# One scheduler step more ahead of two groups of TensorE products in a two-layer hybrid decoder trunk

## The chip, the cores and the metric

The kernel runs on one core of one Trainium2 chip. The metric is the device time of one execution in microseconds (us). Before the change it is 919.61 us, the median of three runs (918.66 to 920.67).

## What is computed

Each of two layers normalises x (256 tokens, 2048 channels), projects it to the inputs of four head groups, computes each group, gates it, and maps the four back through `w_out` with a residual. The change touches the attention groups (fox, moba) and the gated linear attention (gla). Cut from the reference:

```python
def hybrid_layer(x, layer_idx, norm_g, w_in, ..., w_out, rope_diff, rope_moba):
    h = rms_norm(x, norm_g)
    p = split_columns(jnp.einsum("bsd,de->bse", h, w_in))
    fox = forgetting_attention(...)      # softmax(q k^T * scale + F[t] - F[s], causal) v
    diff = differential_attention(...)   # (softmax(q1 k1^T) - lam softmax(q2 k2^T)) v
    moba = moba_attention(...)           # with 256 tokens: one causal block, softmax(q k^T) v
    gla = gla_chunked(...)               # S_t = diag(a_t) S_{t-1} + k_t^T v_t,  o_t = q_t S_t
    mixed = jnp.concatenate([fox, diff, moba, gla], axis=-1)
    return x + jnp.einsum("bse,ed->bsd", mixed, w_out)

def reference(x, ...):
    for l in range(DEPTH):               # DEPTH = 2, SEQ = 256, D_MODEL = 2048
        x = hybrid_layer(x, l, ...)
    return rms_norm(x, final_norm_g)
```

The kernel does not evaluate gla chunk by chunk as the reference does. It splits the 128 tokens of a row block into seven levels (halves, quarters, down to single tokens). At each level the keys of a first half, scaled by their decay to the middle, meet the queries of the second half, scaled by their decay from the middle, in one 128x128 product. These seven are called the **level products** here.

## The kernel before

**The main stream.** All the weights of both layers pass through one loop, `for i, s in enumerate(plan)`. A step holds two 128-row slices of weights, 512 columns wide (some blocks have 348, the last ones 256). An SP DMA brings it to `raw` (four buffers); ScalarE rounds it to `hi`, VectorE subtracts to `lo` (four buffers each, prepared three steps ahead); TensorE multiplies twelve times: both row blocks of x with `hi`, of the low part of x with `hi`, and of x with `lo`. `load` starts the DMA of step i+7 in iteration i, `prepare` the split of step i+3. A layer has 128 steps of `w_in` and 32 of `w_out`, plus the narrow last column block in layer 1. Steps are counted from 0 in this text, and steps of layer 1 from 160.

**The side work.** Everything else (softmax, rotations, gates, gla) is written as Python generators, the tasks. After the twelve multiplications of step i the loop calls `tick`, which runs each task to its next `yield`, unless the estimated cost of VectorE's or ScalarE's side work is over the time that TensorE's work has given (`left`); then the rest of the tasks get no turn in this iteration. So a `yield` puts what follows it one iteration later at least. The order of instructions on every engine is fixed when the program is built, and each engine works its own list in that order. VectorE's side work of iteration i stands behind the `lo` of step i+3, TensorE's behind the multiplications of step i.

**gla (L591).** For each of two pairs of heads it makes seven decays on VectorE (tile `eight`), their exponentials on ScalarE, the scaled queries on VectorE (`tq`, fourteen small products, a `yield` inside), then the scaled keys on VectorE (seven products into `eight`, L654 to 656). After a `yield`, VectorE does two last products for the state (L658, L659), and in that same turn, without a `yield`, TensorE's level products for row block 0 (`matmul(pc[:, i], ee[:, m, i], tq[:, m, i], ...)`, L664) are issued. Row block 1 and the state's product follow one iteration apart. `pcs` and `px` are PSUM tiles named `side`, of which there are two.

**attend (L742), used by fox and moba.** The probabilities of each row block are turned by `turned_p`: a transposition of 32x32 squares on VectorE, four SP DMAs to DRAM (`far`), one POOL DMA back (`four<-far`, or `two<-far` for row block 0), and then four yields (`LANDS`). `attend` waits for both, yields once (L762), and issues twelve products with v (L766 to 770): for each head one from `two` and two from `four`. The result is gated on VectorE and split to `mTh` (ScalarE) and `mTl` (VectorE), the left operands of `w_out`. The first eight steps of `w_out` use the quarters of gla and fox, the next four diff's, and only then, from the thirteenth step (step 140) on, moba's.

**Pools.** Tiles `four` (ten slots), `two` (six), `eight` (one), `side` (two), `far` (six) are handed out in the order in which they come free. A task that finds none waits an iteration.

Of the kernel before, what the change touches and what calls it, by code (L numbers as in the profile page):

```python
# [207 lines left out]
def hybrid_trunk(  # L208
# [83 lines left out]
    def joined(box):  # L292
        while not box:
            yield
        return box[0]
# [295 lines left out]
    def gla(l, an):  # L591
        yield from until("constants")
        ps = yield from take_side()
        for m in range(2):
            transpose(ps[0:16, m * P:(m + 1) * P], an[:, m])
        yield
        v_.tensor_copy(at17[0:16], ps[0:16, 0:256])
        side.put(ps)
        yield
        al = yield from take_side()  # L600
        for pair in range(2):
            matmul(al[:, pair * SEQ:(pair + 1) * SEQ], wa[:, l, pair * P:(pair + 1) * P], at17, True, True)
        yield
        e = yield from s2.take([P, 512])
        gl = yield from s2.take([P, 2, SEQ])
        yield from log_sigmoid(gl.rearrange("p a t -> p (a t)"), al[:, :512], e)
        s2.put(e)
        side.put(al)
        yield

        F = yield from s2.take([P, 2, 2, P])
        for pair in range(2):
            for m in range(2):
                v_.tensor_tensor_scan(F[:, pair, m], one.to_broadcast([P, P]), gl[:, pair, m * P:(m + 1) * P], 0.0,
                                      op0=OP.mult, op1=OP.add)
        s2.put(gl)
        yield from until(("gla_qk", l))
        qkT = env["gla_qk", l]
        dgs = env["dgs", l].rearrange("p m h -> p (m h)")
        sT = yield from s4.take([P, 2, H, P])  # L620
        for c in range(8):
            a_.activation(sT[:, c // 4, c % 4], ident, AF.Copy, scale=dgs[:, c:c + 1])
        sx = yield from s2.take([P, H, P])
        for pair in range(2):
            ee = yield from s8.take([P, 2, NL + 1, P])

            for i, h in enumerate(GLA_LEVELS):
                f = F[:, pair].rearrange("p m (b two h) -> p m b two h", two=2, h=h)
                z = ee[:, :, i].rearrange("p m (b two h) -> p m b two h", two=2, h=h)
                mid = f[:, :, :, 0, h - 1:h].to_broadcast([P, 2, 64 // h, h])  # L630
                v_.tensor_sub(z[:, :, :, 0], mid, f[:, :, :, 0])
                v_.tensor_sub(z[:, :, :, 1], f[:, :, :, 1], mid)
                if i % 3 == 2:
                    yield
            v_.tensor_sub(ee[:, 0, NL], F[:, pair, 0, P - 1:].to_broadcast([P, P]), F[:, pair, 0])
            yield
            a_.activation(ee[:, 0], ee[:, 0], AF.Exp, scale=1.0 / GLA_TAU)
            a_.activation(ee[:, 1, :NL], ee[:, 1, :NL], AF.Exp, scale=1.0 / GLA_TAU)
            a_.activation(ee[:, 1, NL], F[:, pair, 1], AF.Exp, scale=1.0 / GLA_TAU)
            yield  # L640

            def half(z, h, second):
                return z.rearrange("p m (b two h) -> p m b two h", two=2, h=h)[:, :, :, second]

            qv, kv = (qkT.rearrange("p (m c) t -> p c m t", m=2)[:, c] for c in (pair, 2 + pair))
            for i, h in enumerate(GLA_LEVELS):
                for hh in range(2):
                    rows = slice(hh * 64, hh * 64 + 64)
                    v_.tensor_mul(tq[rows, :, i, hh].rearrange("p m (b h) -> p m b h", h=h), half(ee[rows, :, i], h, 1),
                                  half(qv[rows], h, 1))  # L650
                if i == 3:
                    yield
            yield
            for i, h in enumerate(GLA_LEVELS):  # L654
                dst = half(ee[:, :, i], h, 0)
                v_.tensor_mul(dst, dst, half(kv, h, 0))
            yield
            v_.tensor_mul(ee[:, 0, NL], ee[:, 0, NL], kv[:, 0])  # L658
            v_.tensor_mul(ee[:, 1, NL], ee[:, 1, NL], qv[:, 1])  # L659
            for m in range(2):  # L660
                pcs = yield from take_side()
                pc = pcs.rearrange("p (l x c) -> p l x c", l=NL + 1, x=2)
                for i in range(NL):
                    matmul(pc[:, i], ee[:, m, i], tq[:, m, i], True, True)  # L664
                yield
                for i, h in enumerate(GLA_LEVELS):
                    if h >= 32:
                        for k in range(0, P, 2 * h):
                            a_.activation(sT[k:k + h, m, pair * 2:pair * 2 + 2, k + h:k + 2 * h],
                                          pc[k:k + h, i, :, k // 2:k // 2 + h], AF.Copy)  # L670
                        continue
                    dst = sT[:, m, pair * 2:pair * 2 + 2].rearrange("p x (b two h) -> p x b two h", two=2, h=h)[:, :, :, 1]
                    src = pc[:, i].rearrange("p x (b h) -> p x b h", h=h)
                    mk = masks[:, i].rearrange("p (b h) -> p b h", h=h)[:, None].to_broadcast([P, 2, 64 // h, h])
                    v_.copy_predicated(dst, mk, src)
                side.put(pcs)
            px = yield from take_side()
            for hh in range(2):
                rows = slice(hh * 64, hh * 64 + 64)
                matmul(px[:, hh * 512:hh * 512 + P], ee[rows, 0, NL], ee[rows, 1, NL], True, True, tiles=2)  # L680
            s8.put(ee)
            yield
            a_.activation(sx[:, pair * 2:pair * 2 + 2], px.rearrange("p (h t) -> p h t", h=2)[:, :, :P], AF.Copy)
            side.put(px)
        s4.put(qkT)
        s2.put(F)
        yield from until(("gla_v", l))
        yield
        vn = env["gla_v", l]
        ops = yield from take_side()  # L690
        o = ops.rearrange("p (m h d) -> p m h d", m=2, h=H)
        for h in range(H):
            matmul(o[:, 0, h], sT[:, 0, h], vn[:, 0, h * P:(h + 1) * P], True, True)
        for h in range(H):
            matmul(o[:, 1, h], sT[:, 1, h], vn[:, 1, h * P:(h + 1) * P], True, False)
            matmul(o[:, 1, h], sx[:, h], vn[:, 0, h * P:(h + 1) * P], False, True)
        s4.put(sT, vn)
        s2.put(sx)
        yield
        yield from finish_rows(l, 3, o, ops, None, env["gla_sg", l], gng[:, l:l + 1])  # L700
# [41 lines left out]
    def attend(l, gi, name, qT, kT, forget=None):  # L742

        su = sm.tile([P, 2, H], F32, name="su")
        rs = sm.tile([P, 2, H], F32, name="rs")
        boxes = []
        for m, pool in enumerate((s2, s4)):
            p = yield from softmax_part(m, qT, kT, slice(0, P), HD ** -0.5, su, forget)
            if m:
                s4.put(qT, kT[0])  # L750
                if forget is not None:
                    forget.release()
            v_.reciprocal(rs[:, m], su[:, m])
            for h in range(H):
                a_.activation(p[:, h], p[:, h], AF.Copy, scale=rs[:, m, h:h + 1])
            yield
            boxes.append(spawn(turned_p(p, m, partial(pool.put, p))))
        yield from until((name + "_v", l))
        yield from until((name + "_g", l))
        t0, p0 = yield from joined(boxes[0])  # L760
        t1, p1 = yield from joined(boxes[1])
        yield  # L762
        vn, (sgt, sg) = env[name + "_v", l], env[name + "_g", l]
        ops = yield from take_side()
        o = ops.rearrange("p (m h t) -> p m h t", m=2, h=H)
        for h in range(H):  # L766
            v0, v1 = (vn[:, j, h * P:(h + 1) * P] for j in range(2))
            matmul(o[:, 0, h], v0, p0[:, h], True, True)
            matmul(o[:, 1, h], v0, p1[:, 2 * h], True, False)
            matmul(o[:, 1, h], v1, p1[:, 2 * h + 1], False, True)  # L770
        s2.put(t0)
        s4.put(t1, vn)
        yield
        mixed = yield from s4.take([P, 2 * H, P])
        v_.tensor_mul(in_squares(mixed), ops.rearrange("p (x i r) -> p x i r", i=4, r=32), sg)
        side.put(ops)
        s4.put(sgt)
        yield
        yield from split_group(l, gi, mixed)
# [511 lines left out]
```

## Time and profile before

| | |
|---|---|
| median of three runs | 919.61 us |
| the profiled execution: its own time | 920.54 us |
| its span, first to last instruction | 918.8 us |
| TensorE busy | 901.3 us (98%) |
| VectorE busy | 571.5 us (62%) |
| ScalarE busy | 524.6 us (57%) |
| mean granted TensorE clock | 0.995 |
| DMA | 205.34 MB, 223 GB/s over the span |

In the profile PE is TensorE, PEld its weight load, DVE VectorE, ACT ScalarE, SPq SyncE's queue. L178 is the helper through which all VectorE and ScalarE instructions pass, and L276 the one of all matmuls, so the tile names tell them apart: `mm<-hi,hTp` and `mm<-lo,hTp` are main-stream steps (`mTh`, `mTl` in `w_out`), `side<-tq,eight` the level products, `side<-two,four` and `side<-four,four` the products with v. An fp32 matmul that is not split counts as two records. A timeline row has the start, the length, the engine, the instruction and its count; in brackets at its end stands the engine's idle time ahead of it, and what ended it.

### The profile page before, as it was taken

The page shows a single profiled execution, that of the slowest core. Times are in us where ns is not written, and L with a number is a line of the kernel's source. Part 1 is how long each engine was busy: PE and PEld are TensorE (multiplying, and loading weights), DVE is VectorE, ACT ScalarE, POOL GpSimd, SP SyncE. Part 2 cuts the span into 40 slices and gives each one's busy share as a digit, 9 for nine tenths or more (in the row PEclk, how much of TensorE's full clock was granted, in tenths as well). Part 3 has the DMA queues.
Part 4 walks back from the last instruction along what each step waited for, and adds up shares of the span by engine and source line. Part 5 has one row for each costly group of instructions (what it writes and reads, how often), then busy time and mean ns, then how long its engine had stood idle before and what let it go on. Part 6 is the DMA issues. An engine that isn't in the chain of part 4 may idle for free.

```text
span 918.8 us, 12421 instructions
## 1 busy us (share of the span) xinstructions
PE 901.3 (98%) x4490; PEld 766.8 (83%) x4490; DVE 571.5 (62%) x831; ACT 524.6 (57%) x819; POOL 38.6 (4%) x55
## 2 busy tenths in 40 slices
PE   8999999999999999999999999999999999999996
PEld 6988789888888888888899887988888888878886
DVE  6765887566558556555655568856655674565662
ACT  6588654664455556535565784566444654754441
POOL 0000000000000010000000000010000000110000
PEclk9999999999999999999999999999999999999998
DMA  8767656587656947757776466667877687587652
GB/s 264 255 206 263 234 182 240 167 301 263 233 183 205 319 156 236 276 200 259 235 231 212 145 235 194 192 212 213 290 231 228 172 264 274 159 307 254 193 164 92
DMA packets 77455, 205.34 MB, mean 223 GB/s; under 512 B 9265, under 2 KB 29137, under 8 KB 77394
## 3 DMA queue, kind: packets, MB, share of 16 engines
q1 hardware_dynamic: 70496, 183.44, 60.7%
q0 software_dynamic: 5408, 19.40, 6.1%
q10 hardware_dynamic: 1490, 1.71, 0.6%
q8 instruction: 35, 0.57, 0.2%
q14 instruction: 26, 0.21, 0.1%
HBM read 184.07 MB, written 20.45 MB: 223 GB/s over the span
## 4 chain that ended last, share of the span: by engine, by line
PE 86%; DMA 4%; ACT 3%; DVE 2%; issue 2%; SPq 1%; DVEq 0%; POOLq 0%; POOL 0%; ACTq 0%
PE mm L276 77%; PE side L276 9%; DMA four<-far 3%; DMA far<-four 1%; ACT hi L178 1%; ACT four L178 1%; DVE lo L178 1%; SPq L310 1%; DMA raw<-in_weights 1%; ACT L178 0%; DVE four L178 0%; DVE tq L178 0%; DVE eight L178 0%; ACT two L178 0%; DVE two L178 0%
## 5 line engine op out<-in xcount | busy, mean ns | idle before, releaser
L178 DVE TENSOR_TENSOR lo<-raw,hi 128x1024 fp32r<-128x1024 f32 (+1 forms) x316 | 368.4, 1170 | 305.4 <-ACT hi L178 288.5
L178 ACT ACTIVATE hi<-raw 128x1024 fp32r<-128x1024 f32 (+1 forms) x316 | 319.1, 1017 | 301.6 <-PE mm L276 244.1
L276 PE MATMUL mm<-hi,hTp 128*128 128x512 f32 (+1 forms) x1920 | 461.3, 382 | 2.6 <-ACT hi L178 2.6
L276 PEld LDWEIGHTS mm<-hi,hTp 128*128 128x128 f32 x1920 | 352.3, 188 | 68.1 <-ACT hi L178 3.9
L276 PE MATMUL mm<-lo,hTp 128*128 128x512 f32 (+1 forms) x960 | 248.3, 380 | 0.0
L276 PEld LDWEIGHTS mm<-lo,hTp 128*128 128x128 f32 x960 | 177.8, 188 | 32.7
L276 PE MATMUL mm<-hi,mTh 128*128 128x512 f32 (+1 forms) x256 | 64.6, 377 | 0.0
L276 PE MATMUL mm<-hi,mTl 128*128 128x512 f32 (+1 forms) x256 | 64.4, 376 | 0.0
L276 PE MATMUL mm<-lo,mTh 128*128 128x512 f32 (+1 forms) x256 | 64.4, 376 | 0.0
L276 PEld LDWEIGHTS mm<-lo,mTh 128*128 128x128 f32 x256 | 46.2, 188 | 8.8
L276 PEld LDWEIGHTS mm<-hi,mTl 128*128 128x128 f32 x256 | 46.2, 188 | 8.7
L276 PEld LDWEIGHTS mm<-hi,mTh 128*128 128x128 f32 x256 | 46.1, 188 | 8.7
L312 POOL DMA_DIRECT2D four<-far x32 | 17.2, 538 | 617.2 <-DMA far<-four 266.3
L276 PE MATMUL side<-four,four 128*128 128x128 f32 (+1 forms) x320 | 37.3, 277 | 1.9 <-DMA four<-far 1.9
L276 PEld LDWEIGHTS side<-four,four 128*128 128x128 f32 (+1 forms) x320 | 34.1, 190 | 4.6 <-DMA four<-far 2.5
L178 DVE STREAM_TRANSPOSE four<-four 128x1024 f32<-128x1024 f32 x24 | 29.5, 1230 | 0.0
L178 ACT ACT_TABLE_LOAD x22 | 28.2, 1283 | 0.3
L178 ACT ACTIVATE four<-mm,rstd 128x512 f32<-128x512 f32 (+1 forms) x40 | 24.4, 661 | 0.1
L276 PE MATMUL side<-hi,hTp 128*128 128x348 f32 x128 | 22.9, 321 | 0.0
L178 ACT ACTIVATE four<-side 32x64 f32<-32x64 f32 (+2 forms) x28 | 8.8, 342 | 24.3 <-PE side L276 24.3
L276 PEld LDWEIGHTS side<-hi,hTp 128*128 128x128 f32 x128 | 20.8, 188 | 1.3 <-issue 0.7
L178 ACT ACTIVATE four<-side,nb 128x256 f32<-128x256 f32 (+1 forms) x48 | 20.4, 437 | 1.5 <-DVE nb L178 1.2
(135 smaller groups left out, 500.1 us busy)
## 6 DMA issues: line engine op xcount, KB each, us to landing
raw<-in_weights SPq DMA_DIRECT2D x272, 512.0 KB, 4.3
far<-four SPq DMA_DIRECT2D x128, 128.0 KB, 4.2
four<-far POOLq DMA_DIRECT2D x32, 512.0 KB, 6.4
raw<-in_weights SPq DMA_DIRECT2D x47, 348.0 KB, 3.4
xs<-in_x SPq DMA_DIRECT2D x4, 512.0 KB, 5.1
four<-in_xt SPq DMA_DIRECT2D x3, 512.0 KB, 5.6
far<-two SPq DMA_DIRECT2D x24, 64.0 KB, 3.6
two<-far POOLq DMA_DIRECT2D x6, 256.0 KB, 5.2
```

Of the source, the lines that this page charges most:

```text
L178: return f(*args, **kw)
L276: t_.matmul(out, lhsT, rhs, start=start, stop=stop)
L310: nc.sync.dma_start(d[:, :, i].rearrange("j c f -> c j f"), t[32 * i:32 * i + 32].rearrange("c (j f) -> c j f", j=4))
L312: g_.dma_start(t, d.rearrange("j c i f -> (j c) (i f)"))
```

## The change

A `yield` is added at two places. In `gla`, the level products move to the turn after the two last VectorE products, and with them all that follows in the task. In `attend`, the products with v and what follows move one turn back. No instruction is added or taken away in the source.

```diff
@@ -657,6 +657,7 @@ (gla)
             yield
             v_.tensor_mul(ee[:, 0, NL], ee[:, 0, NL], kv[:, 0])
             v_.tensor_mul(ee[:, 1, NL], ee[:, 1, NL], qv[:, 1])
+            yield
             for m in range(2):
                 pcs = yield from take_side()
                 pc = pcs.rearrange("p (l x c) -> p l x c", l=NL + 1, x=2)
@@ -759,6 +760,7 @@ (attend)
         yield from until((name + "_g", l))
         t0, p0 = yield from joined(boxes[0])
         t1, p1 = yield from joined(boxes[1])
+        yield
         yield
         vn, (sgt, sg) = env[name + "_v", l], env[name + "_g", l]
         ops = yield from take_side()
```

TensorE, layer 0, the first pair of heads: `hi_1017` belongs to step 40, `hi_1043` to step 41. Before:

```order
L276 MATMUL mm_1101<-hi_1017,hTp_113 128x512 x8
L276 MATMUL mm_1101<-lo_1018,hTp_113 128x512 x4
L276 MATMUL side1_1116<-tq_94,eight0_900 128x128 x7
L276 MATMUL mm_1101<-hi_1043,hTp_113 128x512 x8
L276 MATMUL mm_1101<-lo_1044,hTp_113 128x512 x4
L276 MATMUL side0_1150<-tq_94,eight0_900 128x128 x7
```

Of the change, at the same place of TensorE's list:

```order
L276 MATMUL mm_1101<-hi_1017,hTp_113 128x512 x8
L276 MATMUL mm_1101<-lo_1018,hTp_113 128x512 x4
L276 MATMUL mm_1101<-hi_1043,hTp_113 128x512 x8
L276 MATMUL mm_1101<-lo_1044,hTp_113 128x512 x4
L276 MATMUL side1_1134<-tq_94,eight0_900 128x128 x7
L276 MATMUL mm_1101<-hi_1067,hTp_113 128x512 x8
```

The first seven level products stand behind step 41 and no longer behind step 40. The seven VectorE products that they read stay where they were, in iteration 39.

VectorE, layer 0, the second pair of heads (`eight0_1213`): from the scaled queries to the scaled keys, with the transposition of fox's keys (`four4_1368`). Before:

```order
L178 TENSOR_TENSOR tq_94<-eight0_1213,four2_870 64x2x64 x8
L178 TENSOR_TENSOR lo_1316<-raw_1225,hi_1315 128x696
L178 TENSOR_TENSOR tq_94<-eight0_1213,four2_870 64x2x64 x6
L178 TENSOR_TENSOR lo_1344<-raw_1249,hi_1343 128x696
L178 TENSOR_TENSOR eight0_1213<-eight0_1213,four2_870 128x2x64
L178 TENSOR_TENSOR eight0_1213<-eight0_1213,four2_870 128x2x2x32
L178 TENSOR_TENSOR eight0_1213<-eight0_1213,four2_870 128x2x4x16
L178 TENSOR_TENSOR eight0_1213<-eight0_1213,four2_870 128x2x8x8
L178 TENSOR_TENSOR eight0_1213<-eight0_1213,four2_870 128x2x16x4
L178 TENSOR_TENSOR eight0_1213<-eight0_1213,four2_870 128x2x32x2
L178 TENSOR_TENSOR eight0_1213<-eight0_1213,four2_870 128x2x64
L178 STREAM_TRANSPOSE four4_1368<-four8_1321 128x1024
```

Of the change (the pair's tile is now `eight0_1232`, the transposed keys `four4_1397`):

```order
L178 TENSOR_TENSOR tq_94<-eight0_1232,four2_870 64x2x64 x8
L178 TENSOR_TENSOR lo_1374<-raw_1288,hi_1373 128x696
L178 TENSOR_TENSOR tq_94<-eight0_1232,four2_870 64x2x64 x6
L178 STREAM_TRANSPOSE four4_1397<-four8_1313 128x1024
L178 TENSOR_TENSOR lo_1400<-raw_1311,hi_1399 128x696
L178 TENSOR_TENSOR eight0_1232<-eight0_1232,four2_870 128x2x64
L178 TENSOR_TENSOR eight0_1232<-eight0_1232,four2_870 128x2x2x32
```

The scaled queries stand in iterations 50 and 51 (before: 47 and 48), the scaled keys in 52 (before: 49), the level products behind step 54 (before: 50). The transposition of fox's keys now comes ahead of the scaled keys. The steps from 48 to 55 are 348 columns wide.

TensorE, layer 0, moba's products with v: `four4_3167` holds the turned probabilities of row block 1, `hi_3255` belongs to step 130, `hi_3274` to step 131. One piece of the difference would be the whole group, so its head is shown, before:

```order
L276 MATMUL mm_3283<-hi_3255,mTl_115 128x512 x4
L276 MATMUL mm_3283<-lo_3256,mTh_114 128x512 x4
L276 MATMUL side1_3333<-two3_3062,four5_3280 128x128
L276 MATMUL side1_3333<-four4_3167,four5_3280 128x128 x2
L276 MATMUL side1_3333<-two3_3062,four5_3280 128x128
```

Of the change:

```order
L276 MATMUL mm_3283<-lo_3256,mTh_114 128x512 x4
L276 MATMUL mm_3283<-hi_3274,mTh_114 128x512 x4
L276 MATMUL mm_3283<-hi_3274,mTl_115 128x512 x4
L276 MATMUL mm_3283<-lo_3275,mTh_114 128x512 x4
L276 MATMUL side1_3351<-two3_3062,four8_3280 128x128
L276 MATMUL side1_3351<-four4_3167,four8_3280 128x128 x2
```

The group stands behind step 131 and no longer behind step 130. Along the whole of TensorE's list the groups of layer 0 move so: first pair's level products by 1 step, the second pair's and gla's output by 4, fox's scores by 4 and 5, fox's products with v by 6 (from behind step 73 to behind step 79), all of diff and moba's scores by 0, moba's products with v by 1. Layer 1 has the same moves. VectorE's transposition of fox's probabilities of row block 1 moves from iteration 65 to 70, so by one step less than the product that reads them.

## Prediction

> **What bounds the kernel now.** I read the page's first and fourth parts, then TensorE's waits, then the timeline at each of them.
>
> ```profile
> PE 901.3 (98%) x4490; PEld 766.8 (83%) x4490; DVE 571.5 (62%) x831; ACT 524.6 (57%) x819; POOL 38.6 (4%) x55
> PE 86%; DMA 4%; ACT 3%; DVE 2%; issue 2%; SPq 1%; DVEq 0%; POOLq 0%; POOL 0%; ACTq 0%
> PE side L276 <- DVE eight L178: 3.0, 2, 1.7
> PE mm L276 <- ACT hi L178: 2.6, 2, 2.1
> PE side L276 <- DMA four<-far: 1.9, 3, 1.0
> ```
>
> TensorE is busy for 98% of the span and carries 86% of the chain that ended last. No work of TensorE is added or removed, so only its idle time can be won. The third row says that level products waited twice for VectorE's `eight`, 3.0 us together; the last, that products with v waited three times for turned probabilities, 1.9 us. These five are what the change moves. The rest of TensorE's idle time is the start, the tail behind its last matmul and one wait for `hi`, and the change reaches none of them.
>
> **The two level-product waits.** Layer 0, first pair, then its second group as the undisturbed pattern, then layer 1's first group:
>
> ```profile
> 109.09 1.07 PE L276 MATMUL mm<-lo,hTp 128*128 128x512 f32 x4
> 111.00 1.49 DVE L178 TENSOR_TENSOR eight<-eight,four 128x128 f32<-128x128 f32 x7
> 111.43 1.80 PE L276 MATMUL side<-tq,eight 128*128 128x128 f32 x14 [1.28 <-DVE eight L178]
> 112.99 2.10 PE L276 MATMUL mm<-hi,hTp 128*128 128x512 f32 x8
> 114.92 1.08 PE L276 MATMUL mm<-lo,hTp 128*128 128x512 f32 x4
> 115.84 1.72 PE L276 MATMUL side<-tq,eight 128*128 128x128 f32 x14
> 117.32 2.10 PE L276 MATMUL mm<-hi,hTp 128*128 128x512 f32 x8
> ...
> 557.99 1.07 PE L276 MATMUL mm<-lo,hTp 128*128 128x512 f32 x4
> 560.76 1.80 PE L276 MATMUL side<-tq,eight 128*128 128x128 f32 x14 [1.70 <-DVE eight L178]
> 562.31 2.10 PE L276 MATMUL mm<-hi,hTp 128*128 128x512 f32 x8
> ```
>
> Ends of matmuls are modelled, starts are not, so I count from start to start. Undisturbed, `lo` to level products takes 115.84 - 114.92 = 0.92, and the group 117.32 - 115.84 = 1.48. In layer 0 these are 2.34 and 1.56, in layer 1 2.77 and 1.55. Lost: 1.42 + 0.08 = **1.50** and 1.85 + 0.07 = **1.92**.
>
> Does one step cure them? Without the wait step 41 starts where the group would have stood, at 109.09 + 0.92 = 110.0, and takes at most 115.84 - 112.99 = 2.85 (the rows of such a step with a restart in it). So the group comes at about 112.85. Its first input was there at 111.43, when it began before; the last of the seven VectorE products ended at 111.00 + 1.49 = 112.49. In layer 1 the group comes at 557.99 + 0.92 + 2.85 = 561.76, against a first input at 560.76, and seven keys take VectorE 1.49, no longer than the group takes. VectorE's products keep their place in its list, so nothing follows TensorE back. Both waits go.
>
> **The three waits for turned probabilities.** First fox in layer 0, which did not wait, then moba in layer 0, fox and moba in layer 1:
>
> ```profile
> 209.08 0.38 PE L276 MATMUL side<-two,four 128*128 128x128 f32 x2
> ...
> 211.68 2.10 PE L276 MATMUL mm<-hi,hTp 128*128 128x512 f32 x8
> ...
> 375.84 0.38 PE L276 MATMUL side<-two,four 128*128 128x128 f32 x2
> 376.83 0.71 PE L276 MATMUL side<-four,four 128*128 128x128 f32 x4 [0.61 <-DMA four<-far]
> ...
> 379.31 1.17 PE L276 MATMUL mm<-hi,mTh 128*128 128x512 f32 x4
> ...
> 382.15 1.07 PE L276 MATMUL mm<-hi,mTh 128*128 128x512 f32 x4
> ...
> 658.41 0.38 PE L276 MATMUL side<-two,four 128*128 128x128 f32 x2
> ...
> 661.58 2.09 PE L276 MATMUL mm<-hi,hTp 128*128 128x512 f32 x8
> ...
> 825.74 0.38 PE L276 MATMUL side<-two,four 128*128 128x128 f32 x2
> 827.11 0.71 PE L276 MATMUL side<-four,four 128*128 128x128 f32 x4 [1.00 <-DMA four<-far]
> ...
> 829.59 1.17 PE L276 MATMUL mm<-hi,mTh 128*128 128x512 f32 x4
> ```
>
> The undisturbed group takes 2.60. The others take 3.47, 3.17 and 3.85: lost **0.87**, **0.57** and **1.25**. The transfer came at most 1.37 after its group began (825.74 to 827.11), and a step is 2.7, so a step more covers it with 1.3 to spare. For fox the transposition moves back by 5 steps and its reader by 6, so there too one step is won.
>
> The sum is 1.50 + 1.92 + 0.87 + 0.57 + 1.25 = **6.1 us**. The idle brackets alone would give 3.0 + 1.9 = 4.9.
>
> The Trainium skill, page "TensorE: Matmul & The Clock Gate", Part 2, "Single matmul latency", says why starts give more: a matmul in a stream hides its fill and drain behind its neighbours, an isolated one pays for them, about 166 ns at full clock. An estimate from that figure is 4.9 + 5 x 0.166 = 5.7 us; the starts above show 1.2 us over the brackets, 0.24 a wait, and the measurement decides.
>
> **What moves with it, and where I cost it at nothing.** In gla's second pair VectorE now has two batches of scaled queries, a transposition, two `lo` and the first scaled key ahead of the level products. The rows of the pair before:
>
> ```profile
> 131.70 1.98 PE L276 MATMUL mm<-hi,hTp 128*128 128x512 f32 x8
> 132.76 2.38 DVE L178 TENSOR_TENSOR tq<-eight,four 64x128 f32<-64x128 f32 x8
> 135.17 0.89 DVE L178 TENSOR_TENSOR lo<-raw,hi 128x696 fp32r<-128x696 f32 x1
> 135.98 1.78 DVE L178 TENSOR_TENSOR tq<-eight,four 64x128 f32<-64x128 f32 x6
> 136.31 1.41 PE L276 MATMUL mm<-hi,hTp 128*128 128x348 f32 x8
> 138.19 1.41 PE L276 MATMUL mm<-hi,hTp 128*128 128x348 f32 x8
> 140.00 1.24 DVE L178 STREAM_TRANSPOSE four<-four 128x1024 f32<-128x1024 f32 x1
> ```
>
> By these VectorE needs 2.38 + 0.89 + 1.78 + 1.24 + 0.89 + 0.28 = 7.5 us to the first scaled key, from 1.1 (as at 131.70 and 132.76) to 1.5 us after step 50's start (ScalarE is late there, with three exponentials and a block's rows in its queue). TensorE's steps 50 to 54 take 5 x 1.88 = 9.4. The margin is 0.4 to 0.8 us, and the later keys come as fast as they are used. So a new wait of 0 is my value; its other end is a further narrow step's length less the margin, about 1.4 a layer, 2.8 in all. It cannot win below nothing, since this pair did not wait before. Behind the moved products on TensorE stand only main steps whose parts are three steps ahead.
>
> Moba's products with v delay `mTl` by a step.
>
> ```profile
> 386.45 1.22 DVE L178 TENSOR_TENSOR mTl<-four,mTh 128x1024 fp32r<-128x1024 f32 x1
> 403.92 1.07 PE L276 MATMUL mm<-hi,mTh 128*128 128x512 f32 x4
> ```
>
> It ends at 387.7 and would end near 390.4; step 140 (the row at 403.92), its first reader, starts 13 us later. Nothing. If that cover were gone, the step would cost its whole 2.7 in each layer. Fox's later products put a gating product and a split beside diff's rotation on VectorE, 2.5 us in three iterations, ahead of the transposition of diff's keys. Their reader stands 7 steps behind it, so this too is hidden. (Both are of the shape of the `mTl` row, 1.22 each.) The SP queue gets fox's gate, four issues, ahead of the probabilities of row block 0; that is the third rival below.
>
> The profiled execution took 920.54, so 914.4 by this sum; the median of the runs is 0.9 lower, 919.61, so I predict **913.5 us**.
>
> **The rivals.**
>
> *A new wait takes part of it back.* Gla's second pair is where: the margin of 0.4 to 0.8 us rests on some fifteen durations, and one queue wait of ScalarE undoes it. For it: VectorE's load in these iterations exceeds TensorE's time. Against it: this pair was as crowded before and did not wait. With 1.1 to 4.2 us lost (its bound of 2.8, and one transfer that still comes 1.4 late, as in the row at 827.11) the time is 914.6 to 917.7.
>
> *The program is not further apart.* A `yield` buys a step only if the producers stay. Where the tick's cost rule hands VectorE's products and the transfers back as well, each wait remains. For it: fox's transposition does go back, by 5 steps of 6. Against it: the first pair's VectorE products and moba's transposition stay. Or the weights' stream sets the end once TensorE is faster; against that stand 223 GB/s in the mean and a single wait for `hi` in the middle of the program. Then the time is 918 to 921.
>
> *The SP queue turns it into a loss.* In iterations 67 and 68 twelve issues for gla's rows, fox's gate and fox's probabilities stand in SP's queue between weight loads; before, eight stood there and eight more later.
>
> ```profile
> 360.28 4.76 SPq L310 DMA_DIRECT2D far<-four  x8
> 362.65 1.06 ACT L178 ACTIVATE hi<-raw 128x1024 fp32r<-128x1024 f32 x1 [1.88 <-DMA raw<-in_weights]
> ```
>
> Eight take 4.8 us, twelve 7.1, and ScalarE already waited 1.88 for weights behind eight, with no wait on TensorE. The parts are three steps, 8.2 us, ahead: from a lateness of 8.2 on TensorE waits, and to be slower by 0.2% it must lose 6.1 + 1.8 = 7.9 in two layers, so weights 12 us late in each. Then the time is 921.5 or more. The issues shown account for 2.3 more than before, so I think it unlikely.
>
> **How the numbers follow.** Forecast 0.62, partly taken back 0.19, no change 0.12, slower 0.07. A change of 0.2%, 1.8 us, is about what a measurement of this kernel tells from none. The first two cases are faster by more: 0.81. The runs before lie 1 us to each side of the median; 913.5 less 1.5 is 912.0, and the upper end takes in the second case, to 918.0. That leaves out 0.19.
>
> **What would show it.** In TensorE's waits the rows for `eight` and `four<-far` are gone or below 0.5 us, the level groups take 1.48 and those with v 2.60 from start to start, and the span is near 912.7. A row for `eight` at a group behind step 54 means the second case; weights as releasers of `hi` in TensorE's waits, the last; waits of the old size at the moved groups, the third. A span cut by less than the waits that went would mean that time was lost in matmuls or tail, which I do not expect.

## The result and the profile after

The changed kernel takes **913.7 us** (median of four runs, 912.04 to 914.79) against 919.61 us before: the ratio is 0.9932, with a 95% interval of 0.9916 to 0.9948. In a later series it took 913.8 us. Its profiled execution took 914.79 us with a span of 913.0 us.

The first and fourth parts of the page of the changed kernel, and then TensorE's waits (engine, instruction, line, what was waited for: us in total, times, the longest):

```profile
PE 901.4 (99%) x4490; PEld 767.8 (84%) x4490; DVE 569.9 (62%) x831; ACT 530.1 (58%) x823; POOL 36.8 (4%) x55
PE 96%; ACT 1%; issue 1%; DMA 0%; DVE 0%; SPq 0%; POOLq 0%; POOL 0%; DVEq 0%; ACTq 0%
```

```profile
PE mm L276 <- ACT hi L178: 2.4, 2, 1.9
PE side L368 <- DVE halfpow L362: 1.2, 1, 1.2
```

TensorE's busy time is the same to 0.1 us, in a span that is 5.8 us shorter, and its share of the chain that ended last rises from 86% to 96%. Both rows that the change aimed at, for `eight` and for `four<-far`, are gone. No row has come in their place.

The timeline of the changed kernel at the five places (start, length, engine, instruction, count): gla's first pair, gla's second pair, then moba in layer 0, fox and moba in layer 1.

```profile
112.07 1.50 DVE L178 TENSOR_TENSOR eight<-eight,four 128x128 f32<-128x128 f32 x7
112.88 1.07 PE L276 MATMUL mm<-lo,hTp 128*128 128x512 f32 x4
113.79 1.72 PE L276 MATMUL side<-tq,eight 128*128 128x128 f32 x14
115.27 2.10 PE L276 MATMUL mm<-hi,hTp 128*128 128x512 f32 x8
...
138.99 2.38 DVE L178 TENSOR_TENSOR tq<-eight,four 64x128 f32<-64x128 f32 x8
145.92 1.49 DVE L178 TENSOR_TENSOR eight<-eight,four 128x128 f32<-128x128 f32 x7
147.15 1.72 PE L276 MATMUL side<-tq,eight 128*128 128x128 f32 x14
...
378.16 0.38 PE L276 MATMUL side<-two,four 128*128 128x128 f32 x2
...
380.76 1.18 PE L276 MATMUL mm<-hi,mTh 128*128 128x512 f32 x4
...
671.59 0.38 PE L276 MATMUL side<-two,four 128*128 128x128 f32 x2
...
674.19 2.09 PE L276 MATMUL mm<-hi,hTp 128*128 128x512 f32 x8
...
824.75 0.38 PE L276 MATMUL side<-two,four 128*128 128x128 f32 x2
...
827.34 1.18 PE L276 MATMUL mm<-hi,mTh 128*128 128x512 f32 x4
```

Read from start to start. In the first pair `lo` to the level products takes 113.79 - 112.88 = 0.91 and the group 115.27 - 113.79 = 1.48: the undisturbed values. The seven keys (112.07, 1.50 long) now end before the group begins. In the second pair the seven keys begin at 145.92, so the first ends near 146.2, and the group starts at 147.15 without a wait: about 0.95 to spare. The three groups with v take 2.60, 2.60 and 2.59.

**Where the 5.8 us of the span come from.** I took three stretches: from the span's start to one early matmul, from there to the end of the last matmul, and the tail behind it. The early matmul, in the timelines of before and of the change:

```profile
55.76 0.38 PE L280 MATMUL side<-ct,an 128*16 128x128 f32 x2
```

```profile
56.83 0.38 PE L280 MATMUL side<-ct,an 128*16 128x128 f32 x2
```

It comes 1.07 later in the profiled execution after. TensorE's last matmul ends at 905.06 in place of 910.02, so the middle stretch is shorter by 910.02 - 905.06 + 1.07 = **6.03**. The tail is 913.0 - 905.06 = 7.9 in place of 8.8.

The middle stretch is the steadiest measure on record. It is 854.26 us in the kernel before and 848.24 in the changed one, and 848.24, 848.21 and 848.22 in three further profiled executions with both yields, from the experiments below (the changed kernel again, five yields, the longer warm-up). The start, in contrast, changes from trace to trace of one kernel (the early matmul comes at 56.83 and 55.84 us in the two traces of the changed kernel), and the last experiment looks at it. The tail is 7.9 us in all seven traces of kernels with an added yield and 8.8 in the two without one. So the shorter tail may belong to the change, but no run shows by which way.

### The profile page after: what moved, and what is told of

Its sections match the earlier page's. It is cut to its first block, busy times and chain, and to the rows that moved or that the text cites. A ratio compares the mean times of both kernels' runs of the same rounds, so it can differ in the third digit from the quotient of the medians.

```text
span 913.0 us, 12423 instructions
## 1 busy us (share of the span) xinstructions
PE 901.4 (99%) x4490; PEld 767.8 (84%) x4490; DVE 569.9 (62%) x831; ACT 530.1 (58%) x823; POOL 36.8 (4%) x55
## 4 chain that ended last, share of the span: by engine, by line
PE 96%; ACT 1%; issue 1%; DMA 0%; DVE 0%; SPq 0%; POOLq 0%; POOL 0%; DVEq 0%; ACTq 0%
PE mm L276 86%; PE side L276 9%; DMA raw<-in_weights 0%; ACT L178 0%; ACT hi L178 0%; ACT two L178 0%; DVE two L178 0%; DVE xs L178 0%; SPq L1093 0%; POOLq L1289 0%; POOL rf L423 0%; ACT four L178 0%; ACT fe L178 0%; DVEq L1289 0%; PE side L280 0%
## 5 line engine op out<-in xcount | busy, mean ns | idle before, releaser
L178 ACT ACTIVATE four<-four 128x1024 f32<-128x1024 f32 x14 | 14.7, 1052 | 8.4 <-DMA four<-far 8.2
```

The costliest lines, as they stand in the source:

```text
L178: return f(*args, **kw)
```

## The experiments

The first three kernels ran in one series, in which the kernel before took 921.50 us (18 runs, 918.33 to 923.58). The other four ran in a second series, in which it took 921.54 (8 runs, 920.11 to 923.35). Ratios are to the kernel before in the same series.

### The yield in gla alone

```diff
--- the changed kernel
+++ gla_only
@@ attend
         t1, p1 = yield from joined(boxes[1])
         yield
-        yield
         vn, (sgt, sg) = env[name + "_v", l], env[name + "_g", l]
```

> The yield in gla alone. Theory 1, the waits are five separate ones and each yield cures its own: the two level-product waits go (1.50 + 1.92 us), fox's wait in layer 1 (0.57) and moba's two (0.87 + 1.25) stay, 919.6 - 3.4 = 916.2 us. Theory 2, the yield in gla also cures fox's wait, because it reorders the transfers ahead of it (fox's gate leaves SP's queue before the probabilities): fox's row in TensorE's waits goes too, moba's two stay at 0.6 and 1.0 us in brackets, 919.6 - 4.0 = 915.6 us. Rival, the gain is a by-product of the shift and not of the waits: the span falls by the change's whole 6 us with moba's waits still there, or not at all.

It took 916.8 us (12 runs, 916.04 to 920.89), ratio 0.9963 (0.9948 to 0.9977). TensorE's waits:

```profile
PE mm L276 <- ACT hi L178: 3.1, 2, 2.5
PE side L276 <- DMA four<-far: 2.8, 2, 2.0
PE side L368 <- DVE halfpow L362: 1.2, 1, 1.2
```

The row for `eight` is gone, as both theories had it. For `four<-far` two waits are left, and both are moba's (0.74 in layer 0, 2.02 in layer 1; before 0.61 and 1.00, so 1.15 more, which is what the time has above theory 2's 915.6). Both theories count from 919.6 us, though; against the 921.50 of its own series this kernel won 4.7. The middle stretch of its trace (55.62 to 907.16) is 851.54 us, 2.72 less than before: close to theory 2's 4.0 less the 1.15. **Fox's wait in layer 1 is gone too, though attend's yield isn't there.** In this kernel fox's transposition and its products with v move by 5 steps each, so the distance in steps is that of before. Layer 1 of the kernel before, and of this one, with the transpositions on VectorE, the issues on SP's queue and the group on TensorE:

```profile
637.58 1.24 DVE L178 STREAM_TRANSPOSE four<-gate 128x1024 f32<-128x1024 f32 x1
638.74 1.20 DVE L178 STREAM_TRANSPOSE four<-four 128x1024 f32<-128x1024 f32 x1
641.46 5.32 SPq L310 DMA_DIRECT2D far<-four  x8
```

```profile
637.15 1.24 DVE L178 STREAM_TRANSPOSE four<-gate 128x1024 f32<-128x1024 f32 x1
639.90 4.28 SPq L310 DMA_DIRECT2D far<-four  x8
646.32 1.23 DVE L178 STREAM_TRANSPOSE four<-four 128x1024 f32<-128x1024 f32 x1
649.28 1.75 SPq L310 DMA_DIRECT2D far<-four  x4
668.68 0.38 PE L276 MATMUL side<-two,four 128*128 128x128 f32 x2
```

Before, the gate's transposition and its four issues stand right ahead of those of the probabilities: the eighth issue ends at 641.46 + 5.32 = 646.78, 11.6 us ahead of the group (658.41). With gla's yield the gate goes ahead by itself, together with four issues of gla's, and the probabilities have four issues of their own that end at 651.03, 17.7 us ahead of the group. So the issues end 6 us earlier against the group, without a step.

That is not yet the margin at the reader. POOL's transfer back starts at 649.78 us before and at 659.25 with gla's yield, only 8.6 and 9.4 us ahead of the group. But it takes 5.0 us to land in place of 9.3, so that the row is there 4.7 us ahead of its first reader (668.90), where it was 0.4 late. With attend's yield alone it takes 8.7 us, with both yields 4.6. It is long where the gate's own transfer back starts 1 or 2 us ahead of it, and short where that starts 12 or 13 us ahead. So it fits that the gate, going ahead, cures the wait, more through POOL's transfers than through SP's queue. It is not shown, for no run moved the gate alone.

Four of the twelve runs took 919.4 to 920.9; none of them was profiled, so what they spent is open.

### The yield in attend alone

```diff
--- the changed kernel
+++ attend_only
@@ gla
             v_.tensor_mul(ee[:, 1, NL], ee[:, 1, NL], qv[:, 1])
-            yield
             for m in range(2):
```

> The yield in attend alone. Theories 1 and 2: the three waits for turned probabilities go (0.87 + 0.57 + 1.25 = 2.7 us), the level products' two stay at 1.3 and 1.7 us in brackets; 919.6 - 2.7 = 916.9 us. If theory 2 holds, the gains of the two yields alone add up to 6.7, 0.6 more than the change's. Rival (by-product of the shift): no relation between the rows that go and the time.

It took 917.12 us (7 runs, 915.5 to 917.53), ratio 0.9957 (0.9940 to 0.9974). The expectation, 916.9, counts from 919.6; against its own series the kernel won 4.4 us where 2.7 were expected. The middle stretch of its trace (54.24 to 905.80) is 851.56 us, 2.70 less than before, as expected. TensorE's waits:

```profile
PE side L276 <- DVE eight L178: 3.0, 2, 1.7
PE mm L276 <- ACT hi L178: 2.7, 2, 2.1
PE side L368 <- DVE halfpow L362: 1.2, 1, 1.2
```

The two waits for `eight` have the size of before, and no wait for `four<-far` is left: one step is enough for all three groups with v. Fox's gain can thus be had from either yield, and only once: the two kernels' 2.72 and 2.70, with the 1.15 that moba's longer waits took from the first, make 6.57, and the change won 6.03, about fox's 0.57 less.

### One step less in attend

The kernel before, without the one yield that it has in attend. Every product with v comes a step earlier.

```diff
--- the kernel before
+++ attend_minus
@@ attend
         t1, p1 = yield from joined(boxes[1])
-        yield
         vn, (sgt, sg) = env[name + "_v", l], env[name + "_g", l]
```

> The opposite of the change in attend: its one yield taken out of the kernel of before, so that the products with v stand one step earlier. If a step of distance is worth 2.7 us until the transfer is covered, each of the four groups loses: fox in layer 0 has 0.6 us to spare and loses 2.1, the other three lose 2.7 more than before: 919.6 + 2.1 + 3 x 2.7 = 929.9 us, with waits of about 2.0, 3.3, 3.0 and 3.7 us in brackets. If a transfer's end follows TensorE (its weights stream, its queues) and not the clock, less: 920 to 926. By the Trainium skill's page TensorE: Matmul & The Clock Gate, Part 1, idle time over a window of about 3.4 us halves the clock again; then the matmuls behind the wait of 3.7 us run at twice their length for some microseconds, 1 to 2 us on top.

It took 935.02 us (4 runs, 930.19 to 938.63), ratio 1.0148 (1.0115 to 1.0182). TensorE's waits, and its timeline at fox in layer 0, which did not wait before:

```profile
PE side L276 <- DMA four<-far: 12.3, 4, 3.7
PE mm L276 <- ACT hi L178: 3.2, 2, 2.7
```

```profile
206.42 0.38 PE L276 MATMUL side<-two,four 128*128 128x128 f32 x2
209.04 1.21 PE L276 MATMUL side<-four,four 128*128 128x128 f32 x4 [2.24 <-DMA four<-far]
210.04 0.63 PE L276 MATMUL side<-two,four 128*128 128x128 f32 x2
...
212.56 0.39 PE L276 MATMUL side<-two,four 128*128 128x128 f32 x2
```

All four groups wait, 2.24, 2.99, 3.72 and 3.33 us: 12.3 in all, near what a step's 2.7 more at each gives. So the transfer is what these groups wait for, and the step is the price. But the span of the profiled execution (938.63 us) is 936.9, 18.1 above that of before, and the waits are only 12.3 - 1.9 = 10.4 of it. The timeline shows the rest: behind the wait a pair of products takes 0.63 us where it takes 0.39 otherwise. The granted clock from 209.09 to 212.51 us is 0.50: TensorE runs at half speed there. The view by stretches of the same kernel (stretch, length, busy us and count of PE, PEld, DVE, ACT and POOL, then PEclk, DMA share and GB/s):

```profile
200.00:230.00 30.00, 27.76 (x128) 23.55 (x127) 14.68 (x20) 11.65 (x12) 1.05 (x2) 0.94 0.69 252
230.00:360.00 130.00, 130.00 (x631) 108.25 (x631) 80.07 (x110) 75.90 (x128) 5.85 (x7) 1.00 0.66 215
360.00:390.00 30.00, 27.01 (x120) 23.03 (x119) 15.47 (x14) 12.32 (x14) 1.58 (x3) 0.89 0.79 280
...
640.00:680.00 40.00, 36.28 (x166) 30.61 (x165) 21.20 (x25) 20.24 (x24) 2.18 (x4) 0.96 0.77 251
820.00:850.00 30.00, 26.67 (x124) 22.57 (x123) 15.90 (x14) 12.62 (x15) 3.70 (x7) 0.94 0.90 315
```

Around each of the four groups the granted clock falls below 1, and between them it is full. 30 x 0.06 + 30 x 0.11 + 40 x 0.04 + 30 x 0.06 = 8.5 us of matmul time are lost, besides the idle time. 10.4 + 8.5 is 18.9, against 18.1; 0.7 of it is counted twice, for 1.4 us of the idle time lie in half-speed stretches. The expectation was 10.3 us over the kernel before, and 1 to 2 on top for the clock. The waits came out so, but the median is 13.5 us over its own series' 921.50: the clock's share was put too low. In the fastest of the four runs, 930.19 us, the mean clock is 0.994 (in the profiled one 0.987).

### Five yields in attend, and eight

The changed kernel, with five and eight yields in attend where the change has added one.

```diff
--- the changed kernel
+++ attend5 (attend8: three more)
@@ attend
         yield
         yield
+        yield
+        yield
+        yield
+        yield
         vn, (sgt, sg) = env[name + "_v", l], env[name + "_g", l]
```

> The change with four more steps of distance in attend (five instead of one). If moba's split products lie under 13 us of cover, as forecast, and distance beyond the transfer's end buys nothing, this is the time of the change: ratio to before 0.993, no row for four<-far or eight in TensorE's waits, and moba's low half is there about 2.5 us ahead of step 140. Rival, later products with v push VectorE and ScalarE work into fuller iterations (fox's to behind step 83, among the rotations of diff's keys): a new wait, 1 to 3 us lost.

> The change with seven more steps of distance in attend. The cover of 13 us is 4.8 steps, so now it is used up: moba's products with v stand behind step 138 and their split is needed by step 140. TensorE waits there in each layer, about 1.5 us for the high and 0.5 us for the low half: 2 x 2.0 = 4.0 us lost against the change, ratio to before about 0.9975, rows for mTh or mTl in TensorE's waits. Rival (the cover is not what matters): the time of the change, or the ratio of before at 1.0 with the wait of a whole 7 steps less 4.8 in each layer, 12 us lost.

With five it took 913.59 us (4 runs, 912.12 to 915.14), ratio 0.9920 (0.9902 to 0.9937): no difference to the change. Moba's `mTl` ends at 397.40 us there, 2.6 ahead of step 140 (400.04), as expected. With eight, 917.88 (6 runs, 916.0 to 918.91), ratio 0.9957 (0.9941 to 0.9973), 4.1 above the changed kernel in the same series (913.8, below). The timeline of the kernel with eight, layer 0, at the first steps of `w_out` that read moba's part:

```profile
399.00 1.18 PE L276 MATMUL mm<-hi,mTh 128*128 128x512 f32 x4
...
402.10 1.04 ACT L178 ACTIVATE mTh<-four 128x1024 fp32r<-128x1024 f32 x1
403.19 1.20 PE L276 MATMUL mm<-hi,mTh 128*128 128x512 f32 x4 [1.18 <-ACT mTh L178]
403.37 1.22 DVE L178 TENSOR_TENSOR mTl<-four,mTh 128x1024 fp32r<-128x1024 f32 x1
404.64 1.20 PE L276 MATMUL mm<-hi,mTl 128*128 128x512 f32 x4 [0.26 <-DVE mTl L178]
```

Now `w_out` catches up with its own operand: `mTh` ends at 403.14 and TensorE goes on at 403.19. Both layers show this wait. So the cover that the prediction put at 13 us, 4.8 steps, is there: four steps more than the change fit in, seven don't. The price beyond it was less than the steps. Seven steps are 19 us, 6 more than the cover, and each layer lost 2.0 (the middle stretch is 852.26 us against 848.24), as the expectation had it. From the start of the group to the end of `mTl` it takes only 8.2 us here (396.41 to 404.59), against 11.0 with five yields (386.44 to 397.40).

### The changed kernel again, and one with a longer warm-up

The changed kernel as it is, in the second series, and beside it one with six more matmuls in the warm-up. The warm-up multiplies constants into a tile that nobody reads, while x is brought in and normalised.

```diff
--- the changed kernel
+++ warm16
-WARM = 10
+WARM = 16
```

> The changed kernel once more, on the chip of this call, as the reference for the three others. Ratio to before 0.993 again; the spread of its runs is that of the start (half-speed clock until 6 to 14 us) and not of waits.

> The change with sixteen warming matmuls ahead of the first step instead of ten. They fill the idle time between the warming matmuls and the first step (1.9 us of waiting for hi in the change's trace), so that the first free-running clock window after the start is busy throughout. If that idle time is why the clock record shows half speed until 12.4 us in the trace of before, 13.7 us in the change's, but full speed from 6.1 us on in that of the yield in attend alone, the half-speed stretch ends by 8 us in every run: 1 to 3 us won against the change in the same call, and a narrower spread. If the window's phase alone decides, no gain.

The changed kernel took 913.8 us (4 runs, 912.04 to 914.06), ratio 0.9912 (0.9896 to 0.9928). With the longer warm-up it is **912.4 us** (4 runs, 912.26 to 912.45), ratio 0.9901 (0.9883 to 0.9919), and the runs lie within 0.2 us where they lay within 2.0. The start in the changed kernel's first trace, and with the longer warm-up (TensorE alone):

```profile
1.20 4.45 PE L368 MATMUL side<-four 128*128 128x512 bf16 x10 [1.20 <-DVE halfpow L362]
7.51 2.69 PE L276 MATMUL mm<-hi,hTp 128*128 128x348 f32 x8 [1.87 <-ACT hi L178]
10.00 1.36 PE L276 MATMUL mm<-lo,hTp 128*128 128x348 f32 x4
```

```profile
1.19 5.82 PE L368 MATMUL side<-four 128*128 128x512 bf16 x16 [1.19 <-DVE halfpow L362]
7.83 1.52 PE L276 MATMUL mm<-hi,hTp 128*128 128x348 f32 x8 [0.81 <-ACT hi L178]
9.19 0.79 PE L276 MATMUL mm<-lo,hTp 128*128 128x348 f32 x4
```

The first eight narrow matmuls take 2.69 us in the one and 1.52 in the other, the next four 1.36 and 0.79: the trace of the changed kernel has half-speed matmuls up to 13.7 us, where its clock record begins, and the trace with the filled gap has the full clock from 5.7 us on. This version has the lowest median here, 1.4 us under the change's 913.8. The two intervals overlap, though, and the changed kernel's fastest runs (912.04) are as fast. What the longer warm-up buys is a start that is good in each of its four runs (mean clock 0.998 in all): the early matmul comes at 54.31 us, and with five yields, which have ten warming matmuls, it came at 54.22 in the profiled run.

## Why the prediction was right

The time, 913.5 us forecast and 913.7 measured, and the case, both kinds of wait gone and no new one, came out as put down. That the two times agree within 0.2 us is partly luck: the tail became 0.8 us shorter, which nobody forecast, the start differs by up to 2.6 us between the traces (54.22 to 56.83), and against the 921.5 us of the later series the change won 7.7. What stands without luck is the middle stretch. Step by step:

- **What bounds the kernel.** That only TensorE's idle time can be won: shown. Its busy time went from 901.3 to 901.4.
- **The level products**, 1.50 and 1.92: shown. The groups stand at the undisturbed 0.91 and 1.48, and with attend's yield alone both waits stay, 3.0 in the brackets.
- **The products with v**, 0.87, 0.57 and 1.25: shown in size. The reason holds for moba, which waits until attend's yield comes (first and second experiment) and waits 2.4 and 2.3 us longer in the brackets, near a step's 2.7, when one is taken away (third).
- **Fox** is the step whose reason was incomplete. The prediction said "for fox the transposition moves back by 5 steps and its reader by 6, so there too one step is won". That step does cure it, alone. But in the changed kernel it was not needed: with gla's yield alone the gate goes ahead of the probabilities by itself, and the wait is gone without a step. The prediction saw the same shift of SP's issues and filed it as a risk, the third rival; it came with a gain.
- **The sum.** 6.1 from start to start; the middle stretch is shorter by 6.02 to 6.05 in all four traces with both yields. The idle brackets (4.9) would have been too small, and so would the estimate from the Trainium skill's page "TensorE: Matmul & The Clock Gate", Part 2 (5.7). The late start (1.07) and the shorter tail (0.8) nearly cancelled, so that the span shows 5.8.
- **The second pair's margin**, forecast 0.4 to 0.8, was about 0.95: no wait there, so the first rival fell. From the scaled queries (138.99) to the first key VectorE took 7.2 us, where the sum of durations had 7.5.
- **Moba's `mTl`** at nothing, with a cover of 13 us: shown from both sides by the kernels with five and eight yields. That a step costs its whole 2.7 once the cover is gone did not come out: 6 us beyond it cost 2.0 in a layer.
- **The rivals.** The second, that the program is not further apart, fell with the groups of moba. The third, SP's queue, fell: in the changed kernel the one wait for `hi` in the middle is as long as before (0.56 and 0.55), and a release by weights appears in no row of TensorE's waits.
- **Not in the prediction** was that a wait on TensorE can cost its clock beside its length. It made no difference here, because the five waits were short (the last section shows how short), but in the other direction, with one step less, it is nearly as large as the waits (8.5 us beside 10.4).

What stays open: the kernel before took 919.6 us in the first series and 921.5 in both later series, while the changed one took 913.7 and 913.8. The kernel before depends on when transfers land and the changed one no longer does, which would fit; but none of the later runs of the kernel before was profiled, so it isn't shown.

## What to carry to other kernels

Where the busiest engine waits for a short time at a few known places, moving the waiting group back by one step of the loop is worth its gap from start to start, if the operands that are made from the group have more cover than a step. Measure that cover in the trace before: up to there a step more cost nothing here, and beyond it a part of its length. A step that is added also moves every transfer that is queued beside it, and this can cure or make a wait elsewhere: look at the queues of both orders, and count the risk in both directions. And try each of two edits alone, for their gains can overlap as they did at fox.

## What the hardware showed that was not expected

**Short idle times already cost TensorE its clock, and it matters where they lie.** The kernel with one step less around fox's wait of 2.24 us in layer 0, the kernel with gla's yield alone around its wait of 2.02 us, and the kernel before around its longest (1.70 us), in the view by stretches:

```profile
205.68:209.09 3.41, 1.17 (x7) 0.83 (x6) 1.86 (x2) 1.59 (x2) 0.00 (x0) 1.00 0.97 365
209.09:212.51 3.42, 3.42 (x16) 3.42 (x17) 0.00 (x0) 0.00 (x0) 0.00 (x0) 0.50 0.64 250
```

```profile
820.07:823.48 3.41, 2.15 (x11) 1.65 (x9) 3.41 (x4) 2.36 (x3) 0.00 (x0) 1.00 1.03 401
823.48:826.89 3.41, 2.65 (x23) 2.65 (x24) 1.68 (x2) 1.06 (x1) 0.00 (x0) 1.00 1.02 405
```

```profile
558.57:561.98 3.41, 1.71 (x14) 1.31 (x13) 3.37 (x11) 0.68 (x1) 0.00 (x0) 1.00 0.53 187
```

The edges of these stretches come from the traces' clock records. In the kernel with one step less the granted clock changes at 11.12, 209.09, 212.51, 379.76, 386.59, 669.89, 673.30, 840.56 and 843.97 us, and all the distances are whole multiples of 3.413 us. In the other traces, too, changes before TensorE's last matmul are whole multiples of 3.413 us apart, each time from another starting point. So the clock seems to be set once in every window of 3.41 us, and the rows above are such windows: 2.24 us idle within one were followed by one at half speed, which is 1.7 us lost; 2.02 us fell on two windows, 1.26 and 0.76, and cost no clock; nor did 1.70 in one.

Up to TensorE's last matmul, in the nine traces, every window at full speed with 2.06 us of idle time or more was followed by one at half speed, and none with 1.70 or less. That covers the start as well. The gap behind ten warming matmuls was 2.12 us with attend's yield alone, 1.64 of it in one window, and the clock stayed full; in the kernel before all of its 2.06 lay in one window, and the next ran at half speed. In the changed kernel's first trace the clock record begins too late to tell. The longer wait isn't always the dearer: with one step less, 2.99 us cost two windows, for 0.91 of it lay in the second, and 3.72 and 3.33 cost one each.

So a gap of about 2 us may or may not cost 1.7 us more than itself, by how it falls on the windows, and their starting point differs from run to run. The Trainium skill's page "TensorE: Matmul & The Clock Gate", Part 1, "HAM oscillation — how this bites in real kernels", gives the rule "no PE-idle gaps >~3.4µs". Here gaps well under that cost clock, by the rows above, so the measurement decides. That the windows by which the gate judges run freely, as the same part says, agrees with the starting points, though no run here set them on purpose.
